# One-layer hybrid encoder block: the pages of the input stage in another order, its dependent steps further apart, a pool's tiles asked for in the old order

## The chip, the cores and the metric

One core of one Trainium2 chip runs the whole block. The metric is the device time of one execution in microseconds, the median of several runs. A core has a matrix engine (PE, whose weight loads are shown apart as PEld), a vector engine (DVE), a scalar engine (ACT), GpSimd (POOL) and a sync engine (SP). Here SP issues most of the loads, POOL issues the loads that add to what is in the tile, and PE, DVE and ACT do the arithmetic.

## The reference, cut to what matters

One layer on 512 tokens of width 2048. Only the first third bears on the change.

```python
h = rms_norm(x, norm_mix_w)
q_a, k_a, v_a, q_g, k_g, v_g, r_g, gate_lr = split_cols(h @ w_in, IN_SPLITS)
y_a = chunked_band_attention(q_a, k_a, v_a, att_rel_bias)        # 16 heads of 64
gate_logit = gate_lr @ w_gla_gate_up + b_gla_gate                # rank 16
log_a = log_sigmoid(gate_logit) / 16
o_g = gated_linear_attention(q_g, k_g, v_g, log_a)               # 4 heads, dv 256
y_g = rms_norm(o_g, gla_norm_w) * silu(r_g)
x = x + concat(y_a, y_g) @ w_out
# then a gated MLP with a causal convolution, and a gated embedding, unchanged here
```

The two values `v_a` and `v_g` are 512 x 1024 each. The per-token factor of `rms_norm` is not applied ahead of the products: they are made from `x * norm_mix_w`, and their results are scaled by the factor afterwards.

## The kernel before, in words

**Products.** Each large product is cut in quarters and made from seven products P1 to P7 instead of eight. Their left operands here are weights (L11, L12, L21, L22 from memory, and sums S1 to S4 of these), and their right operands are quarters of `x` and differences of them (R11, R21, R22, N1, N2, T3, T4). Float32 accuracy comes from splitting both factors into a high and a low float32r part and making three matmuls of them.

**The value stage** (lines 1004 to 1523) is the first of the kernel, and makes `v_g` and `v_a`. Its work is cut into 56 pages, `vpages` in line 1007: 14 steps, each one product of one value, with 4 pages. A page is 128 x 1024 weights, 512 KB. It takes an ACT copy that rounds it to the high part, a DVE subtraction that leaves the low part (`value_split`), and 12 matmuls of 128x512. Tiles named `wvg_..` and `wva_..` are raw pages, `w` is a split page, `in_R` and `in_N` are split operands of `x`, `h` holds split differences, and `vgA`, `vgB`, `vgC`, `vgD`, `vaA` and so on are the accumulators in PSUM (`VALUE_BANKS`, line 1006).

**Where a page comes from.** Pages of P1, P2 and P4 are plain loads by SP. The others hold sums of weights: SP loads L21 (`sum_load`; into the tiles e0 to e3 of the pool `gla` for `v_g`), and POOL issues a load of another block that is added to the tile on arrival (`sum_more`). One such tile is used three times, so the second sum can only be added after the split that read the first. In the trace these added loads are the queue q0, and those of SP are the queue q1.

**What sets the order.** `value_step(n)` (line 1049) issues the load of page n+4 where it is a plain one, splits page n+2, runs the functions that a table gives for step n (lines 1445 to 1501), and then issues the 12 matmuls of page n. The instructions stand on each engine in the order in which this code issues them. The table holds all that has to happen beside the products:

- `x_load` brings pieces of `x`; `left` and `right` split operands of it; `weigh_left`, `differences` and `spread_differences` make and split the others.
- `token_load` and `token_square` sum the squares of the tokens, and `token_norm` (step 26) makes of them the per-token factor: a root, its reciprocal and one Newton step on DVE (`rtok`), a diagonal of it (`dg`, four DVE operations in `rstd_bc`, line 136), a matmul that spreads it over the partitions (`pb`), and a copy to `rb`.
- `collect_first` and `collect_more` take accumulators out of PSUM, `value_done` scales a finished quarter by `rtok` on ACT and stores it to memory by POOL (`vgd`, `vad`).
- The gate of the linear attention: `gate_loads` (30) and `gate_weights` (34) load and split its weights (`g_S`, `gls`), `gate_rank` (35) multiplies them with `x` (64 matmuls, `plr`), `gate_low` (36) scales the result (`lf`, `lr`), `gate_up` (37, 39) makes the logits (`pz`), `gate_exp` and `gate_ln` (40, 41) the logarithm of their sigmoid, and sums, scans and decays follow (42 to 54).

**After the value stage** comes the front stage, with 16 units for the queries, keys and the output gate `r_g` (operand tiles `u`, accumulators `accA` to `accC`). The linear attention runs beside it, and its results are stored to memory as `ond` from the tiles `g_e` (line 1423). Then the pool `gla` is closed and the pool `att` of the softmax attention is opened on the same memory (`open_attention`, line 1533). A tile of the new pool waits for the last use of those tiles of the old one whose place it takes. `attend` (line 646) makes, for each pair of heads, the tiles Q, Kh and Kl (`high` on ACT, `low` on DVE), the scores (`psc` in PSUM), and the score tiles `sc` on DVE and ACT. Where a tile of the pool `gla` lies depends on the order in which its tags are first asked for: before, this was e0, e1, t9, e2, e3, t8, S.

**The output gate's units.** `after_gates` (line 758) multiplies a unit of `r_g` (128 x 1024) by the per-token factor on DVE, applies Silu on ACT and multiplies it by the linear attention's result.

Of the kernel before, what the change touches and what calls it, by code (L numbers as in the profile page):

```python
# [14 lines left out]
P = 128  # L15
# [27 lines left out]
def encoder_block(ctx: ExitStack, tc: tile.TileContext, A, out):  # L43
# [71 lines left out]
    def psum_aux(name):  # L115
        return aux_bank(name)
# [18 lines left out]

    def rstd_bc(rt):
        nt = rt.shape[1]
        dg = tp.tile([P, T], F32, tag="dg", name="dg")
        for t in range(nt):
            vec.tensor_scalar(dg[:, t * P:(t + 1) * P], ident, rt[:, t:t + 1], None, ALU.mult)  # L140
        pb = psum_aux("pb")[:, :nt * P]
        ten.matmul(pb, ones, dg[:, :nt * P], start=True, stop=True)
        return pb
# [739 lines left out]

    for i, f in enumerate(sum_chores(summed[:4])):
        agenda[11 + 5 * i].append((0, f))
# [121 lines left out]
    vpages = [(v, p, j) for v, p in VALUE_STEPS for j in range(4)]  # L1007
# [120 lines left out]

    def gate_loads():
# [32 lines left out]
    def x_load(kt, c):  # L1162
        syn.dma_start(xslot(kt, "")[:, c], A["x"][kt][:, c])
# [21 lines left out]
    mixed = {}  # L1185

    def differences(k, names):
# [3 lines left out]
        for name in names:  # L1191
# [4 lines left out]
            elif name == "N2":  # L1196
                place = ("sq", "dg", "acc", "sq", "dg", "sq", "acc", "dg")[k]
                mixed[k] = acc if place == "acc" else tp.tile([P, T], F32, tag=place, name="mixed")
# [26 lines left out]
    def token_norm():  # L1225
        token_roots(rtok)
        act.activation(rb, rstd_bc(rtok), AF.Copy)
# [216 lines left out]
    first_half, second_half = ("N1", "N2", "T4"), ("T4", "N2")  # L1444
    for n, *fs in (
            (0, (left, 2), (left, 3), *((x_load, k, hi_tokens) for k in (0, 1, 2))),
            (1, (left, 4), (left, 5), *((x_load, k, hi_tokens) for k in (3, 4, 5))),
            (2, (left, 6), (left, 7), *((x_load, k, hi_tokens) for k in (6, 7)), (x_load, 8, all_tokens)),
            (3, (x_load, 9, all_tokens), (x_load, 10, all_tokens), (weigh_left, 0), (weigh_left, 1)),
            (4, (x_load, 11, all_tokens), (x_load, 12, all_tokens), (differences, 0, first_half), (weigh_left, 2)),  # L1450
            (5, (x_load, 13, all_tokens), (x_load, 14, all_tokens), (right, 0, 0), (spread_differences, 0, *second_half), (right, 1, 0)),
            (6, (x_load, 15, all_tokens), (differences, 1, first_half), (weigh_left, 3)),
            (7, (right, 2, 0), (right, 3, 2), (spread_differences, 1, *second_half)),
            (8, (right, 4, 0), (right, 5, 0), (differences, 2, ("N1",)), (weigh_left, 4), (sum_load, "g", 0)),
            (9, (right, 6, 2), (right, 7, 2), (differences, 2, ("N2", "T4")), (weigh_left, 5)),
            (10, (spread_differences, 2, *second_half), (differences, 3, ("N1", "N2")), (weigh_left, 6), (sum_load, "g", 1)),
            (11, (differences, 3, ("T4",)), (spread_differences, 3, *second_half), (weigh_left, 7)),
            (12, (collect_first, "g", "C11", "A"), (collect_more, "g", "C11", "B"), (sum_load, "g", 2), (sum_more, "g", "P5", 0, "L22")),
            (13, (differences, 4, first_half), (sum_more, "g", "P5", 1, "L22")),
            (14, (spread_differences, 4, *second_half), (differences, 5, ("N1", "N2")), (sum_load, "g", 3)),  # L1460
            (15, (differences, 5, ("T4",)), (spread_differences, 5, *second_half), (sum_more, "g", "P5", 2, "L22")),
            (16, (differences, 6, first_half), (spread_differences, 6, "T4"), (sum_more, "g", "P5", 3, "L22"), (token_load, 0)),
            (17, (differences, 7, first_half), (spread_differences, 7, "T4"), (token_load, 1)),
            (18, (spread_differences, 0, "N1"), (spread_differences, 1, "N1"), (differences, 7, ("T3",)), (token_load, 2), (token_square, 0)),
            (19, (collect_first, "a", "C11", "A"), (collect_more, "a", "C11", "B"), (spread_differences, 2, "N1"),
             (differences, 3, ("T3",)), (spread_differences, 3, "N1", "T3"), (token_load, 3), (token_square, 1), (sum_more, "g", "P6", 0, "L11")),
            (20, (spread_differences, 4, "N1"), (spread_differences, 5, "N1"), (spread_differences, 7, "N1", "T3"), (differences, 6, ("T3",)), (token_load, 4), (token_square, 2),
             (sum_more, "g", "P6", 1, "L11")),
            (21, (collect_first, "g", "C21", "D", -1), (spread_differences, 6, "N1", "T3"),
             (token_load, 5), (token_square, 3), (sum_more, "g", "P6", 2, "L11")),  # L1470
            (22, *((differences, k, ("T3",)) for k in (0, 1, 2)), (token_load, 6), (token_square, 4), (sum_more, "g", "P6", 3, "L11")),
            (23, *((differences, k, ("T3",)) for k in (4, 5)), (token_load, 7), (token_square, 5), (sum_more, "g", "P3", 0, "L12")),
            (24, (collect_first, "g", "C22", "C", -1), (spread_differences, 6, "N2"), (spread_differences, 7, "N2"), (token_square, 6),
             (sum_more, "g", "P3", 1, "L12"), (value_load, "g", "P7", 0)),
            (25, (token_square, 7), (spread_differences, 0, "T3"), (spread_differences, 1, "T3"), (sum_more, "g", "P3", 2, "L12"),
             (value_load, "g", "P7", 1)),
            (26, (token_norm,), (right, 0, 1), (right, 1, 1), (sum_more, "g", "P3", 3, "L12"), (value_load, "g", "P7", 2),
             (sum_more, "g", "P7", 0, "L11")),
            (27, (right, 2, 1), (right, 4, 1), (value_done, "g", "C11"), (sum_more, "g", "P7", 1, "L11")),
            (28, (collect_first, "g", "C12", "A"), (right, 5, 1), (value_done, "a", "C11"), (use_rings, {"wr": ("r3", "r0", "r1", "r2")}),  # L1480
             (value_load, "g", "P7", 3), (sum_more, "g", "P7", 2, "L11")),
            (29, (spread_differences, 2, "T3"), (sum_load, "a", 0)),
            (30, (spread_differences, 4, "T3"), (spread_differences, 5, "T3"), (sum_more, "g", "P7", 3, "L11"), (gate_loads,)),
            (31, (sum_load, "a", 1)),
            (32, (collect_more, "g", "C12", "C"), (value_done, "g", "C12"), (sum_more, "a", "P5", 0, "L22")),
            (33, (sum_load, "a", 2)), (34, (gate_weights,), (sum_more, "a", "P5", 1, "L22")),
            (35, (gate_rank,), (sum_load, "a", 3)),
            (36, (collect_more, "g", "C21", "A"), (collect_more, "g", "C22", "A"), (value_done, "g", "C21"), (value_done, "g", "C22"),
             (gate_low,)),
            (37, (gate_up, (0, 1)), (gate_abs, (0, 1)), (gate_min, (0, 1))), (38, (sum_right, "a", 2)),  # L1490
            (39, (gate_up, (2, 3)), (gate_abs, (2, 3)), (gate_min, (2, 3)), (sum_right, "a", 3)),
            (40, (collect_first, "a", "C21", "D", -1), (gate_exp, (0, 1, 2, 3))), (41, (gate_ln, (0, 1, 2, 3))),
            (42, (gate_sum, (0, 1))), (43, (gate_scan, (0,)), (gate_sum, (2, 3))), (44, (collect_first, "a", "C22", "C", -1), (gate_scan, (1,))),
            (45, (gate_scan, (2,))), (46, (gate_scan, (3,))), (48, (collect_first, "a", "C12", "A")),
            (52, (collect_more, "a", "C12", "C"), (value_done, "a", "C12")),
# [4 lines left out]
            *((47 + i, (gate_decay, (i,))) for i in range(4)), *((51 + i, (gate_small, (i,))) for i in range(4)), (54, (linear_pages,)),  # L1500
# [6 lines left out]
    for k in (1, 2, 3):  # L1507
        x_load(k, lo_tokens)
    value_load("g", "P1", 1, 2)
    for k in (4, 5):  # L1510
        x_load(k, lo_tokens)
    value_load("g", "P1", 2)
    for k in (6, 7):
        x_load(k, lo_tokens)
# [3 lines left out]
    value_load("g", "P1", 3)  # L1518
# [284 lines left out]
```

## Time and profile before

| what | us |
|---|---|
| median of the runs (lowest and highest) | 2256.96 (2256.66 to 2257.14) |
| the profiled execution | 2257.45 |
| its span, first to last instruction | 2255.4 |
| PE busy in the span | 2188.2 (97%) |
| DVE, ACT, POOL busy | 1875.4, 1351.0, 227.1 |
| mean granted clock of PE | 0.986 |

The profiled execution is 0.5 us above the median, and 2.05 us of it lie outside the span. A row of a timeline gives the start, the time, the engine, the line, the operation, the result and operand tiles and the shape, with a count of equal instructions in a row; in brackets stands how long the engine sat idle ahead of it and what ended that. Nearly all rows name line 62, a helper that records every operation, so they are told apart by their tiles. A row of the windows gives the busy time of each engine in a stretch, the granted clock of PE as a share of full speed, and the busy share and rate of the DMA engines. The matrix engine is idle almost nowhere but in the value stage and at a few places of the front stage.

### The profile page before, as it was taken

What the parts mean: (1) busy time and instruction counts of PE and PEld (TensorE: products, weight loads), DVE (VectorE), ACT (ScalarE), POOL (GpSimd) and SP (SyncE); (2) the same over time, 40 slices, a digit from 0 to 9 for tenths busy, and PEclk for the clock granted to TensorE, in tenths of its full rate; (3) what the DMA queues carried; (4) which work ended last, traced back from release to release, by engine and by line L of the source; (5) the groups of instructions that cost most, each with busy time, mean ns of one, the idle gap of its engine ahead of it and who ended that gap; (6) DMA issues with size and microseconds to landing.
All of it is one profiled execution on the core that took longest, in us unless ns stands there. A gap on an engine that the chain in (4) does not pass through costs nothing.

```text
span 2255.4 us, 45743 instructions
## 1 busy us (share of the span) xinstructions
PE 2188.2 (97%) x18224; PEld 2134.9 (95%) x18224; DVE 1875.4 (83%) x2581; ACT 1351.0 (60%) x2018; POOL 227.1 (10%) x277
## 2 busy tenths in 40 slices
PE   8779998999999999999999999999999999999997
PEld 7568998899999999999999999999999999999997
DVE  6646787888778898999888888888888787898997
ACT  6647456777576575555555555555564464666765
POOL 0221101011010001111111110000000101000000
PEclk9889999999999999999999999999999999999998
DMA  9979787788998898999999997877876886979996
GB/s 301 254 200 219 212 228 213 213 230 242 263 350 255 272 320 235 293 300 296 291 285 289 271 253 222 212 226 212 233 292 164 257 240 171 337 239 338 292 295 200
DMA packets 205222, 576.08 MB, mean 255 GB/s; under 512 B 22384, under 2 KB 66672, under 8 KB 205008
## 3 DMA queue, kind: packets, MB, share of 16 engines
q1 hardware_dynamic: 166064, 437.70, 54.9%
q0 software_dynamic: 36960, 132.66, 31.1%
q8 instruction: 143, 2.34, 0.4%
q10 hardware_dynamic: 1984, 2.79, 0.3%
q14 instruction: 71, 0.58, 0.1%
HBM read 499.67 MB, written 119.54 MB: 275 GB/s over the span
## 4 chain that ended last, share of the span: by engine, by line
PE 74%; DVE 8%; DMA 8%; ACT 5%; issue 3%; SPq 0%; POOL 0%; DVEq 0%; ACTq 0%; POOLq 0%
PE accA L62 38%; PE accC L62 19%; PE accB L62 10%; DVE w L62 3%; ACT w L62 2%; PE vaA L62 1%; DVE u L62 1%; DMA wvg_P_r<-in_w_v_g 1%; DVE h L62 1%; DMA s<-in_w_up 1%; PE py L62 1%; PE vgA L62 1%; DMA ond<-g_e 1%; DVE s L62 1%; PE psc L62 1%
## 5 line engine op out<-in xcount | busy, mean ns | idle before, releaser
L62 PE MATMUL accA<-h,w 128*128 128x256 f32 x5088 | 615.9, 278 | 5.4 <-ACT u L62 4.5
L62 PEld LDWEIGHTS accA<-h,w 128*128 128x128 f32 x5088 | 596.8, 188 | 8.7 <-ACT u L62 5.4
L62 DVE TENSOR_TENSOR w<-s,w 128x1024 fp32r<-128x1024 f32 (+1 forms) x381 | 457.5, 1201 | 77.6 <-ACT w L62 76.8
L62 PE MATMUL accC<-h,w 128*128 128x256 f32 x4248 | 510.5, 277 | 0.0
L62 PEld LDWEIGHTS accC<-h,w 128*128 128x128 f32 x4248 | 495.6, 188 | 0.3
L62 DVE TENSOR_TENSOR w<-l,w 128x1024 fp32r<-128x1024 f32 (+1 forms) x320 | 382.9, 1196 | 64.2 <-ACT w L62 63.7
L62 ACT ACTIVATE w<-l 128x1024 fp32r<-128x1024 f32 (+1 forms) x320 | 332.1, 1039 | 172.0 <-PE accC L62 114.4
L62 ACT ACTIVATE w<-s 128x1024 fp32r<-128x1024 f32 (+1 forms) x381 | 394.8, 1037 | 22.2 <-PE accB L62 9.8
L62 ACT ACTIVATE u<-accA 128x256 f32<-128x256 f32 x302 | 114.1, 378 | 355.2 <-PE accA L62 355.1
L62 DVE TENSOR_TENSOR s<-s,l 128x1024 f32<-128x1024 f32 (+1 forms) x176 | 211.2, 1200 | 13.1 <-DMA s<-in_w_blk 8.6
L62 POOL DMA_DIRECT2D s<-in_w_up x84 | 73.0, 869 | 719.6 <-DMA s<-in_w_up 402.8
L62 DVE SCALAR_TENSOR_TENSOR cv<-u,cw,cv 128x511 f32<-128x511 f32 (+1 forms) x176 | 131.5, 747 | 3.1
L62 PE MATMUL accA<-up_R,w 128*128 128x256 f32 x1056 | 127.0, 276 | 0.0
L62 PE MATMUL accB<-up_R,w 128*128 128x256 f32 x1056 | 126.8, 276 | 0.0
L62 PE MATMUL accA<-up_N,w 128*128 128x256 f32 x1056 | 126.8, 276 | 0.1
L62 PEld LDWEIGHTS accA<-up_R,w 128*128 128x128 f32 x1056 | 123.0, 188 | 0.5 <-issue 0.5
L62 PEld LDWEIGHTS accA<-up_N,w 128*128 128x128 f32 x1056 | 122.9, 188 | 0.2 <-ACT u L62 0.2
L62 PEld LDWEIGHTS accB<-up_R,w 128*128 128x128 f32 x1056 | 123.1, 188 | 0.0
L62 DVE TENSOR_TENSOR u<-u,rb 128x1024 f32<-128x1024 f32 (+1 forms) x74 | 84.0, 1135 | 18.4 <-ACT u L62 18.2
L62 ACT ACTIVATE u<-accC 128x256 f32<-128x256 f32 x98 | 37.3, 380 | 95.9 <-PE accC L62 95.8
L62 ACT ACTIVATE cv<-u,cw 128x512 f32<-128x512 f32 x88 | 67.1, 810 | 29.7 <-DVE u L62 29.7
L62 DVE TENSOR_TENSOR u<-u,accC 128x256 f32<-128x256 f32 x102 | 42.6, 418 | 50.4 <-PE accC L62 50.0
(368 smaller groups left out, 2973.8 us busy)
## 6 DMA issues: line engine op xcount, KB each, us to landing
l<-in_w_up SPq DMA_DIRECT2D x132, 512.0 KB, 6.6
s<-in_w_up SPq DMA_DIRECT2D x84, 512.0 KB, 6.1
s<-in_w_up POOLq DMA_DIRECT2D x84, 512.0 KB, 7.8
l<-in_w_dn SPq DMA_DIRECT2D x56, 448.0 KB, 5.1
l<-in_w_blk SPq DMA_DIRECT2D x48, 512.0 KB, 5.5
s<-in_w_blk SPq DMA_DIRECT2D x32, 512.0 KB, 4.6
s<-in_w_blk POOLq DMA_DIRECT2D x32, 512.0 KB, 8.1
l<-in_w_out SPq DMA_DIRECT2D x28, 512.0 KB, 4.5
```

The source lines that it names most:

```text
L62: ins = f(*args, **kw)
```

## The change: what it does

**Pages of P1 in turn.** The first eight pages were four of `v_g` and then four of `v_a`; now they alternate. Since both values use the same two pieces of `x` for page j, the pieces are needed every second page. The first loads are reordered to match (x1, a page of `v_a`, x2, x3, a page of `v_g`), and the other pieces of `x` are spread over the steps 0 to 9.

**Dependent steps apart.** `token_norm` becomes four entries: the root and `rtok` at step 27, the diagonal at 28, the matmul `pb` at 30, the copy to `rb` at 32. The gate's weights go from step 34 to 36, its 64 matmuls from 35 to 39, `gate_low` from 36 to 41, `gate_up` from 37 and 39 to 43 and 45, exponential and logarithm from 40 and 41 to 48 and 49, the scans from 43 to 46 to 50 to 54. `value_done` of the first two quarters goes from 27 and 28 to 29 and 30, so on POOL the added loads of the P7 pages 0, 1 and 2 now stand ahead of their four stores, and that of page 3 stands behind them. Operands of later products are made later (`spread_differences` for N2, `right` for R22, and T3), and the tiles `mixed` lie elsewhere.

**Tiles in the old order.** All tags of the pool `gla` are asked for once at its start, in the order t9, t8, S, e0, e1, e2, e3.

**Output gate.** `scale_gate` multiplies three quarters of a unit of `r_g` by the per-token factor six steps into the unit, and `after_gates` is left with 128 x 256.

On PE, at the start of the value stage (`vgA` and `vaA` are the accumulators of P1 for `v_g` and `v_a`, `in_R` the two operand tiles for the pieces 0 to 3 and 4 to 7 of `x`):

```order
-L62 MATMUL vgA<-w,in_R_244 128x512 x24
-L62 MATMUL vgA<-w,in_R_284 128x512 x24
-L62 MATMUL vaA<-w,in_R_244 128x512 x24
-L62 MATMUL vaA<-w,in_R_284 128x512 x24
-L62 MATMUL vgB<-w,in_R_378 128x512 x12
+L62 MATMUL vgA<-w,in_R_246 128x512 x12
+L62 MATMUL vaA<-w,in_R_246 128x512 x12
+L62 MATMUL vgA<-w,in_R_246 128x512 x12
+L62 MATMUL vaA<-w,in_R_246 128x512 x12
+L62 MATMUL vgA<-w,in_R_305 128x512 x12
+L62 MATMUL vaA<-w,in_R_305 128x512 x12
```

The second operand tile was needed after 24 matmuls, and is now needed after 48.

On PE, further on, from the products P6 of `v_g` (`vgA<-w,h`) to the gate's matmuls (`plr`), before:

```order
L62 MATMUL vgA<-w,h_103 128x512 x24
L62 MATMUL pb<-dg,ones 128x512
L62 MATMUL vgA<-w,h_103 128x512 x24
L62 MATMUL vgC<-w,in_R_378 128x512 x12
L62 MATMUL vgC<-w,in_R_423 128x512 x12
L62 MATMUL vgC<-w,in_N_446 128x512 x12
L62 MATMUL vgC<-w,in_N_473 128x512 x12
L62 MATMUL vgA<-w,h_103 128x512 x36
L62 MATMUL plr<-in_R_244,g_S 128x256 x8
```

and now:

```order
L62 MATMUL vgA<-w,h_103 128x512 x48
L62 MATMUL vgC<-w,in_R_376 128x512 x12
L62 MATMUL vgC<-w,in_R_423 128x512 x12
L62 MATMUL pb<-dg,ones 128x512
L62 MATMUL vgC<-w,in_N_473 128x512 x12
L62 MATMUL vgC<-w,in_N_498 128x512 x12
L62 MATMUL vgA<-w,h_103 128x512 x48
L62 MATMUL vaD<-w,h_103 128x512 x36
L62 MATMUL plr<-in_R_246,g_S 128x256 x8
```

`pb` moved behind four more pages, and `plr` behind four more.

On DVE, in the softmax attention's first pair of heads, with what each row waits for (DMAHW is a load or store issued by SP or ACT), before:

```order
L62 SCALAR_TENSOR_TENSOR Q_3140<-u,Q_3140 64x512 [waits Activation_49]
L62 TENSOR_TENSOR Kl_3144<-u,Kh_3142 64x512 [waits DMAHW6_49,DMAHW5_49,Activation_49]
L62 SCALAR_TENSOR_TENSOR Q_3141<-u,Q_3141 64x512 [waits DMAHW0_49,Activation_49]
L62 TENSOR_TENSOR Kl_3145<-u,Kh_3143 64x512 [waits DMAHW4_49,Activation_49]
L62 TENSOR_TENSOR u<-u,accB 128x256 [waits PE_49]
L62 TENSOR_TENSOR s_3190<-s_3190,l_2972 128x1024 [waits DVE_49]
L62 ISA sc,mx<-psc,bias 128x512 [waits PE_49]
```

and now:

```order
L62 SCALAR_TENSOR_TENSOR Q_3165<-u,Q_3165 64x512 [waits Activation_49]
L62 TENSOR_TENSOR Kl_3169<-u,Kh_3167 64x512 [waits Activation_49]
L62 SCALAR_TENSOR_TENSOR Q_3166<-u,Q_3166 64x512 [waits DMAHW3_49,Activation_49]
L62 TENSOR_TENSOR Kl_3170<-u,Kh_3168 64x512 [waits DMAHW7_49,Activation_49]
L62 TENSOR_TENSOR u<-u,accB 128x256 [waits PE_49]
L62 TENSOR_TENSOR s_3215<-s_3215,l_2997 128x1024 [waits DVE_49]
L62 ISA sc,mx<-psc,bias 128x512 [waits DMAHW5_49,DMAHW4_49,PE_49]
```

The wait for two transfers (numbers 6 and 5 before, and 5 and 4 now, since the count is shifted by one) went from the first Kl to the first score tile, ten rows further on. On ACT the same two left the row of the second Kh. The rest of the instructions after the value stage, `scale_gate` aside, stand in the order in which they stood.

The diff, cut to its core:

```diff
-    vpages = [(v, p, j) for v, p in VALUE_STEPS for j in range(4)]
+    vpages = [(v, "P1", j) for j in range(4) for v in "ga"] + [(v, p, j) for v, p in VALUE_STEPS[2:] for j in range(4)]
...
+    for tag, cols_ in (("t9", 1024), ("t8", T), ("S", 768), *((f"e{i}", 1024) for i in range(4))):
+        gt(tag, cols_)
...
+    def scale_gate(unit):
+        vec.tensor_tensor(unit.o[:, 0], unit.o[:, 0], rb, ALU.mult)
+        vec.tensor_tensor(unit.o[:, 1, 256:T], unit.o[:, 1, 256:T], rb[:, 256:T], ALU.mult)
+
+    for u in front.units[12:]:
+        agenda[base[u] + 6].append((1, lambda u=u: scale_gate(u)))
...
-        return [(0, 0, load), (0, 1, lambda: vec.tensor_tensor(unit.o, unit.o, rb2, ALU.mult)),
+        r = rb[:, 0:256]
+        return [(0, 0, load), (0, 1, lambda: vec.tensor_tensor(unit.o[:, 1, 0:256], unit.o[:, 1, 0:256], r, ALU.mult)),
...
-    def token_norm():
-        token_roots(rtok)
-        act.activation(rb, rstd_bc(rtok), AF.Copy)
+    def token_spread():
+        G["dg"] = tp.tile([P, T], F32, tag="dg", name="dg")
+        for t in range(TT):
+            vec.tensor_scalar(G["dg"][:, t * P:(t + 1) * P], ident, rtok[:, t:t + 1], None, ALU.mult)
+
+    def token_bank():
+        G["pb"] = psum_aux("pb")
+        ten.matmul(G["pb"], ones, G["dg"], start=True, stop=True)
+
+    def token_out():
+        act.activation(rb, G["pb"], AF.Copy)
...
-            (26, (token_norm,), (right, 0, 1), (right, 1, 1), (sum_more, "g", "P3", 3, "L12"), (value_load, "g", "P7", 2),
...
+            (27, (token_roots, rtok), (differences, 3, ("T3",)), (differences, 0, ("T3",)), (sum_more, "g", "P7", 1, "L11")),
```

More of the change, by code (lines that the diff above doesn't have):

```diff
@@ L134, in token_roots @@
         vec.scalar_tensor_tensor(dst, t, 1.5, y, ALU.add, ALU.mult)
[L136 to L143, printed above, removed]
     w_all = hp.tile([P, 6 * 1024 + 136], F32R, name="w")
@@ L1443, in encoder_block, with x_rest @@
     lo_tokens, hi_tokens, all_tokens = slice(0, 256), slice(256, T), slice(0, T)
-    first_half, second_half = ("N1", "N2", "T4"), ("T4", "N2")
+    def x_rest(k):
+        x_load(k, hi_tokens)
+        x_load(k + 8, all_tokens)
     for n, *fs in (
[L1446 to L1464, printed above, removed]
@@ new lines, in encoder_block @@
+            (0, (left, 2), (left, 3), (x_load, 4, lo_tokens), (x_load, 5, lo_tokens)),
+            (1, (x_rest, 0)), (2, (left, 4), (left, 5), (x_load, 6, lo_tokens), (x_load, 7, lo_tokens)), (3, (x_rest, 1), (weigh_left, 0)),
+            (4, (x_rest, 2), (left, 6), (left, 7), (differences, 0, ("N1", "N2", "T4")), (weigh_left, 1)),
+            (5, (x_rest, 3), (right, 0, 0), (right, 1, 0), (spread_differences, 0, "T4", "N2")),
+            (6, (x_rest, 4), (differences, 1, ("N1", "N2", "T4")), (weigh_left, 2)),
@@ new lines, in encoder_block @@
+            (7, (x_rest, 5), (right, 2, 0), (right, 3, 0), (spread_differences, 1, "T4", "N2")),
+            (8, (x_rest, 6), (differences, 2, ("N1", "N2", "T4")), (weigh_left, 3)),
+            (9, (x_rest, 7), (right, 4, 0), (right, 5, 0), (spread_differences, 2, "T4"), (sum_load, "g", 0)),
+            (10, (right, 6, 0), (right, 7, 0), (differences, 3, ("N1", "N2")), (weigh_left, 4), (sum_load, "g", 1)),
+            (11, (differences, 3, ("T4",)), (differences, 4, ("N1", "N2")), (weigh_left, 5)),
@@ L1471, in encoder_block @@
[L1471 to L1476, printed above, removed]
@@ new lines, in encoder_block @@
+            (24, (spread_differences, 7, "N2"), (right, 1, 1), (differences, 7, ("T3",)), (token_square, 6), (sum_more, "g", "P3", 1, "L12"),
+             (value_load, "g", "P7", 0)),
+            (25, (collect_first, "g", "C22", "C", -1), (spread_differences, 7, "T3"), (right, 7, 1), (right, 2, 1), (token_square, 7),
+             (sum_more, "g", "P3", 2, "L12"), (value_load, "g", "P7", 1)),
+            (26, (right, 3, 1), (right, 4, 1), (right, 5, 1), (sum_more, "g", "P3", 3, "L12"), (value_load, "g", "P7", 2),
@@ L1487, in encoder_block @@
[L1487 to L1492, printed above, removed]
@@ new lines, in encoder_block @@
+            (38, (sum_right, "a", 2)), (39, (gate_rank,), (sum_right, "a", 3)),
+            (41, (collect_first, "a", "C21", "D", -1), (gate_low,)), (43, (gate_up, (0, 1))),
+            (45, (collect_first, "a", "C22", "C", -1), (gate_abs, (0, 1)), (gate_min, (0, 1)), (gate_up, (2, 3))),
+            (47, (gate_abs, (2, 3)), (gate_min, (2, 3))), (48, (gate_exp, (0, 1, 2, 3))),
+            (49, (collect_first, "a", "C12", "A"), (gate_ln, (0, 1, 2, 3)), (gate_sum, (0, 1))), (50, (gate_scan, (0,)), (gate_sum, (2, 3))),
@@ L1499, in encoder_block @@
             *((43 + j, (sum_more, "a", "P3", j, "L12")) for j in range(4)),
-            *((47 + i, (gate_decay, (i,))) for i in range(4)), *((51 + i, (gate_small, (i,))) for i in range(4)), (54, (linear_pages,)),
+            *((51 + i + (i > 1), (gate_decay, (i,))) for i in range(3)), (55, (gate_decay, (3,)), (gate_small, (0, 1, 2, 3))), (54, (linear_pages,)),
             *((n, (give, tag)) for n, tag in ((47, "r4"), (48, "r5"), (51, "r0"), (52, "r1"), (53, "r2"), (54, "r3")))):
@@ L1506, in encoder_block @@
     value_load("g", "P1", 0, 2)
[L1507 to L1514, printed above, removed]
+    x_load(1, lo_tokens)
+    value_load("a", "P1", 0)
+    x_load(2, lo_tokens)
+    x_load(3, lo_tokens)
+    value_load("g", "P1", 1)
     value_split(0, 2, lambda: left(0))
@@ L1517, in encoder_block @@
     value_split(1)
-    value_load("g", "P1", 3)
+    value_load("a", "P1", 1)
     for n in range(len(vpages)):
```

53 lines of the change are left out of this document (36 added, 17 removed).

## The prediction

> **What bounds the kernel now.** The page's first part gives PE 97% of the span, so time can only be won where PE stands still. The windows over the value stage come first (columns: stretch, length, busy time and count of PE, PEld, DVE, ACT, POOL, granted clock, DMA share, GB/s).
>
> ```profile
> 0.00:10.00 10.00, 7.43 (x34) 6.10 (x34) 2.61 (x6) 4.61 (x7) 1.44 (x11) 1.00 0.78 245
> 10.00:20.00 10.00, 6.77 (x20) 4.99 (x21) 5.16 (x8) 5.13 (x9) 0.00 (x0) 0.66 0.98 333
> 20.00:60.00 40.00, 40.00 (x178) 33.15 (x177) 33.60 (x50) 27.86 (x40) 3.58 (x4) 1.00 0.95 313
> 60.00:80.00 20.00, 15.18 (x59) 11.43 (x58) 15.05 (x26) 12.72 (x24) 2.55 (x3) 0.91 0.86 224
> 80.00:90.00 10.00, 10.00 (x46) 8.29 (x45) 8.24 (x12) 9.26 (x17) 3.10 (x4) 1.00 1.00 256
> 90.00:100.00 10.00, 0.98 (x5) 0.49 (x4) 4.99 (x14) 6.15 (x10) 2.01 (x3) 0.65 1.06 275
> 100.00:120.00 20.00, 20.00 (x80) 15.75 (x81) 9.30 (x13) 12.01 (x20) 6.32 (x8) 0.92 0.98 257
> 120.00:140.00 20.00, 11.51 (x52) 9.96 (x51) 7.70 (x10) 7.45 (x13) 3.34 (x4) 0.76 0.96 281
> 140.00:160.00 20.00, 15.31 (x80) 13.12 (x79) 7.44 (x10) 7.61 (x11) 5.35 (x8) 0.84 0.37 121
> 160.00:213.00 53.00, 51.97 (x224) 41.98 (x223) 33.87 (x44) 36.89 (x51) 12.40 (x15) 0.99 0.95 207
> ```
>
> Two things stand here at once. PE is idle and at a reduced clock in several stretches, and the DMA engines are nearly full in all but one (0.37 from 140 to 160). The timeline of PE names the stalls; the third row gives the full-speed price.
>
> ```profile
> 5.76 3.30 PE L62 MATMUL vgA<-w,in_R 128*128 128x512 f32 x12 [0.43 <-ACT in_R L62]
> 13.20 10.80 PE L62 MATMUL vgA<-w,in_R 128*128 128x512 f32 x36 [4.14 <-ACT in_R L62]
> 23.83 11.04 PE L62 MATMUL vaA<-w,in_R 128*128 128x512 f32 x48
> 34.71 5.60 PE L62 MATMUL vgB<-w,in_R 128*128 128x512 f32 x24
> ...
> 72.92 12.53 PE L62 MATMUL vgC<-w,h 128*128 128x512 f32 x48 [3.76 <-DVE g_t L62]
> ...
> 99.90 2.08 PE L62 MATMUL pb<-dg,ones 128*128 128x512 f32 x2 [9.02 <-DVE dg L62]
> ...
> 135.60 5.37 PE L62 MATMUL plr<-in_R,g_S 128*128 128x256 f32 x24 [8.49 <-DVE g_S L62]
> 140.81 1.12 PE L62 MATMUL plr<-in_N,g_S 128*128 128x256 f32 x8
> 141.77 1.10 PE L62 MATMUL plr<-in_R,gls 128*128 128x256 f32 x8
> ...
> 155.90 1.22 PE L62 MATMUL pz<-lr,g_t 128*128 128x512 f32 x2 [4.69 <-ACT lr L62]
> 156.92 7.66 PE L62 MATMUL vaD<-w,h 128*128 128x512 f32 x24
> 164.41 0.63 PE L62 MATMUL pz<-lr,g_t 128*128 128x512 f32 x2
> ...
> 213.12 2.90 PE L62 MATMUL accA<-in_R,w 128*128 128x256 f32 x24
> ```
>
> 48 matmuls take 34.71 - 23.83 = 10.88 us, so a page of 12 takes 2.72 and 56 pages 152.3. The gate's 64 `plr` matmuls cost about 7.7 (8 in 0.96), `pb` and `pz` about 1. That is 161 us of work between 5.76 and 213.12, which is 207.4: 46.4 us are lost. The five stalls above make 4.14 + 3.76 + 9.02 + 8.49 + 4.69 = 30.1 of it; the rest is mostly the clock after them (36 matmuls after the first took 10.63 us instead of 8.16).
>
> Three of the five are dependent steps set too close: `pb` waits for `dg`, made in the same step; `plr` for the gate's split weights; `pz` for `lr`, two steps after `plr`.
>
> The other large place is the first pair of heads of the softmax attention.
>
> ```profile
> 353.23 1.34 ACTq L1423 DMA_DIRECT2D ond<-g_e  x2
> ...
> 359.50 2.99 PE L62 MATMUL accA<-in_R,w 128*128 128x256 f32 x24
> 368.39 1.28 ACT L62 ACTIVATE Kh<-u 64x512 fp32r<-64x512 f32 x2 [10.38 <-DMA ond<-g_e]
> 368.43 0.68 DVE L62 TENSOR_TENSOR Kl<-u,Kh 64x512 fp32r<-64x512 f32 x1 [9.79 <-DMA ond<-g_e]
> ...
> 370.80 1.22 PE L62 MATMUL accB<-in_R,w 128*128 128x256 f32 x4 [8.31 <-ACT w L62]
> ...
> 376.09 0.46 PE L62 MATMUL psc<-Kh,Q 128*128 128x512 f32 x1
> ...
> 378.23 0.68 DVE L62 CUSTOM_DVE_ANT_0 sc<-psc,bias 128x512 f32<-128x512 f32 x1
> ```
>
> The new tiles Kh and Kl lie where `g_e` lay, whose store was issued at 353.23 and landed at 368.4. The page split for `accB` stands behind them on ACT, so PE waits 8.31 us, and the 24 matmuls of `accB` then take 5.29 us (370.80 to 376.09).
>
> **The change part by part.** *Pages in turn.* The second half of `in_R` is needed after four pages instead of two, 5.4 us later on PE. The 4.14 us stall and its clock go, and page 4 can start 5 us earlier (23.83 to about 18.5). But from 10 to 60 us the transfers run at 0.95 to 0.98, so PE then overtakes its pages and hands most of this back. I count none of it by itself.
>
> *Steps apart.* The diagonal itself is short:
>
> ```profile
> 98.97 0.88 DVE L62 TENSOR_SCALAR dg<-ident,rtok 128x128 f32<-128x128 f32 x4
> ```
>
> `pb` gets two steps between `dg` and itself (5.4 us; `dg` takes 0.88), `plr` three after the weights' split, `pz` two after `lr`. By PE alone 9.02, 8.49 and 4.69 go, and about 2 us of clock after each (24 matmuls after `pz` took 7.49 instead of 5.44). What each leaves behind: the same pages must have arrived earlier. So the stage's sum goes by the transfers.
>
> ```profile
> 0.00:213.00 213.00, 179.15 (x764) 145.25 (x765) 127.94 (x190) 129.68 (x197) 40.08 (x59) 0.91 0.89 245
> ```
>
> 0.89 of 213 is 189.6 us of DMA work, and the change removes no byte of it. In the long full stretches the share is 0.95 to 1.0. At 0.97 the work takes 195.5 us, so the stage ends 17.6 us earlier. Upper bound: no idle transfer at all, 23.4. Lower bound: only the stall whose stretch had free transfers, `pz`, goes: 4.69 and 2.05 of clock, 6.7. I take 17.6, since 0.95 is what the longest stretches without a large stall show (20 to 60, 160 to 213) and 0.98 to 1.06 those from 80 to 120. The free transfers that are left to fill lie almost all in the stretch at 0.37 (12.6 of the 23.4 us), which follows `plr` and holds `pz`.
>
> [...]
>
> *POOL's queue.* Before, the first stores of the values stood ahead of the added loads.
>
> ```profile
> 108.21 1.49 POOL L62 DMA_DIRECT2D vgd<-g_t  x2 [9.37 <-ACT g_t L62]
> 109.69 0.96 POOL L62 DMA_DIRECT2D wvg_P_r<-in_w_v_g  x1
> ```
>
> The load at 109.69 waited behind a store that waited 9.37 us for ACT. Now three of four go ahead, and only P7's page 3 stands behind four stores: it may come a few us late, once. Its cover is the two pages before it (5.4 us). It is inside the lower bound.
>
> *Added and moved work.* The gate's ACT and DVE operations come eight to nine steps later, between page splits, and number as many as before. `gate_exp` and `gate_ln` fall beside the collection of an accumulator at step 49; I take 0, bound 3 us, inside the 0.97. Its results are used after the stage.
>
> *Pool order.* Kh and Kl no longer wait. PE wins 8.31 and, at 2.72 for 24 matmuls, 2.57 of clock: 10.9. The same store is now waited for by `sc`. Without the stall `sc` would start at 378.23 - 10.9 = 367.3, and the store landed at 368.4. I subtract this 1.1 and another 0.8, since DVE's next page splits stand behind `sc`: 9. Bounds 6 (landing 4 us later) and 11.
>
> *Output gate.*
>
> ```profile
> 597.46 1.22 DVE L62 TENSOR_TENSOR u<-u,rb 128x1024 f32<-128x1024 f32 x1
> 598.71 1.06 ACT L62 ACTIVATE u<-u 128x1024 f32<-128x1024 f32 x1 [2.79 <-DVE u L62]
> 599.67 0.36 ACT L62 ACTIVATE u<-accA 128x256 f32<-128x256 f32 x1
> ...
> 600.09 4.27 PE L62 MATMUL accA<-h,w 128*128 128x256 f32 x24 [2.96 <-ACT u L62]
> ```
>
> Here PE waits 2.96 us for a chain that begins with 1.22 us on DVE; a quarter of that work remains, so 0.8 to 0.9 us go at this unit, little at the others. I take 1 (0 to 2: the clock after it may recover too). The three quarters done earlier fill DVE time beside PE.
>
> Sum: 17.6 + 9 + 1 = 27.6. From the profiled 2257.45 that is 2229.85, and as the median lies 0.5 below that execution, 2229.4.
>
> **The rivals.** *Transfers keep their time.* The first pages come sooner, but loads and added loads follow one another through few buffers, and the stage only wins the 6.7 us of `pz`. For it: shares of 0.95 to 1.06 beside the stalls of `pb` and `plr`. Against: PE's stall holds the buffers, so these transfers fetch ahead for later. 6.7 + 9 + 1 = 16.7: 2240.2. Chance 0.22.
>
> *Everything closes.* Transfers are never idle and the store has landed when `sc` comes: 23.4 + 11 + 2 = 36.4, 2220.5. Chance 0.12.
>
> *PE's own work binds.* If better order also made the transfers cheaper than 189.6, all 46.4 go: with 9 and 1, 2200.5. [...] Chance 0.02.
>
> *The store's wait moves.* The pages behind `sc` are fetched earlier, crowd the store of `ond`, and it lands 6 us later: the 9 become 3, 2235.4. Nothing of the landing on ACT's side is changed, which speaks against it. Chance 0.12.
>
> *No change.* `pb` and `plr` wait as long at the new places, since their inputs wait for the same late tokens and pages: within 4.5 us of before. Chance 0.03.
>
> *Slower: the clock.* PE, now ahead, waits for each page of steps 4 to 19, and stays at the low clock there. Price: 24 matmuls in 5.29 instead of 2.72, so 2.57 a page. It decides from (27.6 + 4.5) / 2.57 = 13 pages on; with all 16, 41 us are lost and the time is 2270. For it: after one 4.14 us gap the granted clock was 0.66 for a whole window. Against: PE was busy for 40.00 of 40 us from 20 to 60 at 0.95 of the transfers, so gaps there would be short. Chance 0.03.
>
> [...]
>
> **How the numbers follow.** The forecast has 0.46. The range runs from 2220.5 (upper bounds 23.4, 11 and 2) to 2244.3 (lower bounds 6.7, 6 and 0), rounded to 2220 and 2244.5; it holds the first, second and fourth case. 0.2%, about what a measurement of this kernel can tell, is 4.5 us. Faster by more: 0.46 + 0.22 + 0.12 + 0.02 + 0.12 = 0.94. Within: 0.03. Slower: 0.03.
>
> **What would show it.** Right: `accA` after the value stage starts near 195 instead of 213; `pb`, `plr` and `pz` wait under 1 us; the window that had 0.37 is at 0.9; Kh starts right after Q and `sc` waits for the store by 1 to 2 us. The first rival is right if the three waits are gone but PE waits as long for `w` (ACT, DVE, behind a load). Wrong altogether: `accA` starts after 207, or `accB` still waits over 5 us.

## The result, and the profile after

| | us |
|---|---|
| before, median of 4 (range) | 2257.05 (2256.66 to 2260.32) |
| changed, median of 4 (range) | 2232.44 (2231.36 to 2236.55) |
| ratio, 95% interval | 0.9891, 0.9874 to 0.9908 |
| the changed kernel's profiled execution, its span | 2236.55, 2234.8 |

The change saves 24.6 us (20.8 to 28.4 by the interval); 27.6 were forecast. Of the twelve runs of the pages in turn alone, below, three took 2430, 2443 and 12077 us, far longer than the other nine, and are left out of its median. The profiled execution is 4.1 us above the median of its runs, so its traces explain 20.6 us (span 2255.4 to 2234.8).

The windows of the changed kernel over the value stage, with the columns as before:

```profile
20.00:60.00 40.00, 39.79 (x176) 32.48 (x175) 34.05 (x56) 26.88 (x41) 3.59 (x4) 1.00 1.02 331
...
100.00:120.00 20.00, 15.55 (x60) 12.01 (x59) 8.89 (x14) 10.10 (x17) 6.29 (x9) 0.89 1.05 325
120.00:140.00 20.00, 20.00 (x115) 17.68 (x115) 13.37 (x16) 9.61 (x16) 8.49 (x12) 0.94 0.80 248
140.00:160.00 20.00, 14.83 (x66) 11.92 (x64) 8.62 (x8) 10.70 (x15) 4.20 (x5) 1.00 1.06 235
160.00:200.00 40.00, 37.03 (x157) 29.40 (x157) 23.19 (x25) 27.47 (x41) 6.49 (x8) 0.92 0.63 152
...
0.00:197.00 197.00, 176.96 (x764) 142.29 (x764) 125.20 (x186) 128.45 (x203) 39.42 (x59) 0.97 0.92 262
```

The transfers now run full from 20 to 120 us (1.05 and 1.06 from 60 to 100) and from 140 to 160 us; the share can read slightly above 1, so it is no exact measure. The stretch that had 0.37 is at 1.06, and the free time has moved to 120 to 140 us (0.80) and behind 160 us (0.63). The timeline of PE shows which waits went and which are new.

```profile
97.02 1.10 PE L62 MATMUL pb<-dg,ones 128*128 128x512 f32 x2 [1.70 <-DVE dg L62]
...
115.76 0.79 PE L62 MATMUL vgA<-w,h 128*128 128x512 f32 x1 [3.98 <-ACT w L62]
117.02 5.06 PE L62 MATMUL vgA<-w,h 128*128 128x512 f32 x11 [0.47 <-DVE w L62]
...
130.28 3.01 PE L62 MATMUL plr<-in_R,g_S 128*128 128x256 f32 x24
...
148.75 0.63 PE L62 MATMUL pz<-lr,g_t 128*128 128x512 f32 x2
...
160.92 1.45 PE L62 MATMUL pz<-lr,g_t 128*128 128x512 f32 x2 [6.09 <-DVE g_e L62]
...
197.39 3.00 PE L62 MATMUL accA<-in_R,w 128*128 128x256 f32 x24 [0.68 <-ACT w L62]
...
206.67 4.62 PE L62 MATMUL accA<-h,w 128*128 128x256 f32 x24 [3.56 <-ACT u L62]
211.13 2.89 PE L62 MATMUL accC<-h,w 128*128 128x256 f32 x24
```

`plr` and the first `pz` no longer wait, and `pb` waits 1.70 us instead of 9.02. Three waits are new: 3.98 us for P7's last page of `v_g`, 6.09 us at the second `pz`, and 3.56 us for `u` just after the stage, with a low clock behind it (24 matmuls in 4.46 us, to 211.13, at a granted clock of 0.62). `accA` starts 15.7 us earlier than before. Of this, 10.8 are left at `accC`, which before stood as in the first of these rows (timeline of PE, the kernel before; the second is a mark for the attention):

```profile
221.89 2.88 PE L62 MATMUL accC<-h,w 128*128 128x256 f32 x24
...
423.85 1.25 PE L62 MATMUL py<-PT,va 128*64 128x128 f32 x12 [0.80 <-ACT PT L62]
```

The softmax attention's beginning in the timeline of the changed kernel:

```profile
346.84 1.27 ACT L62 ACTIVATE Kh<-u 64x512 fp32r<-64x512 f32 x2
...
351.28 0.64 PE L62 MATMUL accB<-in_R,w 128*128 128x256 f32 x4
...
354.11 0.39 PE L62 MATMUL psc<-Kh,Q 128*128 128x512 f32 x1
...
357.53 0.69 DVE L62 CUSTOM_DVE_ANT_0 sc<-psc,bias 128x512 f32<-128x512 f32 x1 [0.23 <-DMA ond<-g_e]
...
376.96 1.25 PE L62 MATMUL py<-PT,va 128*64 128x128 f32 x12 [1.61 <-ACT PT L62]
...
404.77 1.25 PE L62 MATMUL py<-PT,va 128*64 128x128 f32 x12 [0.79 <-ACT PT L62]
```

Kh starts without a wait, `accB` follows at full speed (24 matmuls in 2.83 us, at a granted clock of 1.00), and `sc` waits 0.23 us for the store. At `psc` the kernel is 376.09 - 354.11 = 22.0 us ahead, at the `py` of 404.77 still 19.1: some 3 us come back in between, where PE waits for PT (1.61 instead of 0.76 us) and then runs 24 matmuls at a low clock (4.44 us instead of 2.86, at a granted clock of 0.62).

To compare kernels by their parts, three marks serve: the first `accA`, the first `accC`, and the `py` just shown, since whole times scatter. The kernel before ran from 2251.18 to 2264.32 us in the 17 runs beside the first experiments. The kernels of the table are explained in the experiments.

| profiled execution of | accA | accC | py |
|---|---|---|---|
| before | 213.12 | 221.89 | 423.85 |
| changed | 197.39 | 211.13 | 404.77 |
| changed, again | 197.23 | 210.97 | 404.19 |
| pool's order alone | 213.34 | 223.69 | 417.45 |
| pages in turn alone | 216.11 | 226.18 | 431.49 |
| steps apart alone | 200.25 | 213.99 | 416.12 |
| changed, output gate in one piece | 199.15 | 212.91 | 405.28 |
| changed, the gate's last steps later | 200.35 | 211.55 | 407.88 |

The last two run the changed kernel's code up to the last page of the value stage, so `accA` of one and the same stage wanders by 3 us, from 197.2 to 200.4. The products P6 of `v_g` already start at 76.6 to 80.5 us in the four profiles of this stage. From `accA` to `accC`, before and the pool's order alone have the same code too, and take 8.8 and 10.4 us. From `py` to the end of the span, where only the output gate differs, the eight take 1824.8 to 1832.4 us. The runs come from several chips; how much of this is the chip and how much chance stays open.

### The profile page after: what moved, and what is told of

It reads as the page before. It is cut to its first block, busy times and chain, and to the rows that moved or that the text cites. A ratio compares the mean times of both kernels' runs of the same rounds, so it can differ in the third digit from the quotient of the medians.

```text
span 2234.8 us, 45776 instructions
## 1 busy us (share of the span) xinstructions
PE 2186.1 (98%) x18224; PEld 2132.7 (95%) x18224; DVE 1876.8 (84%) x2599; ACT 1352.2 (61%) x2028; POOL 227.0 (10%) x277
## 4 chain that ended last, share of the span: by engine, by line
PE 78%; DVE 7%; DMA 7%; ACT 4%; issue 3%; POOL 0%; SPq 0%; DVEq 0%; ACTq 0%; POOLq 0%
PE accA L62 41%; PE accC L62 20%; PE accB L62 11%; DVE w L62 2%; ACT w L62 1%; DVE h L62 1%; DMA s<-in_w_blk 1%; DMA wvg_P_r<-in_w_v_g 1%; DVE u L62 1%; DMA g_e<-in_w_v_g 1%; PE psc L62 1%; PE py L62 1%; DMA ond<-g_e 1%; PE ptr L62 1%; PE po L62 1%
## 5 line engine op out<-in xcount | busy, mean ns | idle before, releaser
L62 DVE TENSOR_TENSOR u<-u,rb 128x1024 f32<-128x1024 f32 (+2 forms) x82 | 84.9, 1040 | 18.5 <-ACT u L62 18.3
```

The costliest lines, as they stand in the source:

```text
L62: ins = f(*args, **kw)
```

## The experiments

Theory: in the value stage the transfers set the pace, so a stall that goes is only worth the transfer time that was idle beside it. Rivals: the stalls simply add up; or one late transfer or one badly placed step is the bound.

**The changed kernel again.**

> The changed kernel once more, unaltered. Its profiled execution was 2236.55 us while the three others took 2231.4 to 2232.9. If the 4 us between them are a late page of the value stage, a second profile near 2232 us shows less waiting there (PE's waits at pz, 6.1 us, and at the last page of P7 of v_g, 4.0 us) and the same waits after the stage. If they are elsewhere, the waits of the value stage are the same within 1 us.

Measured: 2235.46 us, its profiled execution 2238.32. The waits of the stage are the same (6.39 at `pz`, 3.63 at P7's page, `accA` at 197.23). The marks repeat to 0.6 us here, though not in the other kernels with this stage. The second profile fell on the longest of its five executions again, so no profile shows one of the shorter ones, and where the 4 us between them lie stays open.

**Pool's order alone**, the only edit to the kernel before:

```diff
+    for tag, cols_ in (("t9", 1024), ("t8", T), ("S", 768), *((f"e{i}", 1024) for i in range(4))):
+        gt(tag, cols_)
```

> The kernel before with only the order in which the tiles of the pool gla are asked for. Theory (the store's wait goes from Kh and Kl to sc, where it is nearly over, but the pages behind the attention then come no earlier): PE's 8.3 us at accB go and about 3 us come back within the next 50 us, net 8 us, 2249 us. Rival 1 (all of it stays): 11 us, 2246 us. Rival 2 (the store's wait only moves, and what the changed kernel won there it won because the stage before it ended earlier): under 3 us, 2254 us or more.

Measured: 2245.39 us, ratio 0.9949 (0.9934 to 0.9965). The timeline of PE:

```profile
362.96 2.88 PE L62 MATMUL accA<-in_R,w 128*128 128x256 f32 x24
365.69 0.62 PE L62 MATMUL accB<-in_R,w 128*128 128x256 f32 x4
...
417.45 1.25 PE L62 MATMUL py<-PT,va 128*64 128x128 f32 x12 [0.71 <-ACT PT L62]
```

`accB` follows `accA` at once. From `accC` to `py` it wins (423.85 - 221.89) - (417.45 - 223.69) = 8.2 us; the changed kernel wins 8.3 there. So the wait did not just move, and the part is independent of the stage. All the kernels bear it out: with the order of before, the profiles take 202.0 to 205.3 us from `accC` to `py`, and with the new one 191.1 to 193.8, where the gate's last steps don't fall between. The theory's 8 holds; the 11.5 us of the whole time fit the first rival, but by the marks 3 of them are from elsewhere.

**Pages in turn alone** (the edit is the line of `vpages`, the first loads and the steps 0 to 9 for pieces of `x`):

> The kernel before with only the pages of P1 in turn and the first loads to match; the dependent steps stay close. Theory (transfers set the pace from 10 to 130 us, so PE overtakes its pages and waits later instead): the first stall of 4.1 us goes, the stall at pb grows by about as much, and under 2 us are left, 2255 to 2257 us. Rival (stalls simply add): 6 us, 2251 us.

Measured: 2259.35 us (nine runs), ratio 1.0009 (0.9996 to 1.0022).

```profile
18.18 2.88 PE L62 MATMUL vgA<-w,in_R 128*128 128x512 f32 x12
...
41.42 2.89 PE L62 MATMUL vgB<-w,in_N 128*128 128x512 f32 x6 [2.58 <-ACT in_N L62]
...
73.25 7.07 PE L62 MATMUL vgC<-w,h 128*128 128x512 f32 x18 [3.75 <-DVE g_t L62]
...
100.23 2.08 PE L62 MATMUL pb<-dg,ones 128*128 128x512 f32 x2 [7.67 <-DVE dg L62]
```

The fifth page starts at 18.18 instead of 23.83, yet `vgC` starts at 73.25 (before 72.92): all of it is given back within 55 us, first at a wait for a late piece of `x`. `accA` is 3 us later than before, as much as it wanders in the changed stage. Nothing is gained alone, as the theory says, though the stall at `pb` shrank rather than grew.

**Steps apart alone** (the changed kernel with the old order of P1, of the pool's tiles and of the output gate):

> The changed kernel with P1 in the old order and the old first loads, the pool's tiles in the order of before, and the output gate as before: only the dependent steps are apart. Theory (transfers bind, and the steps apart let them run through): most of the stage's gain is here, accA after the stage starts 10 to 14 us earlier than before, and 4 to 5 us come back at once at the gate's late operations, net 7 to 10 us, 2247 to 2250 us. Rival 1 (stalls add): 20 us or more, 2237 us. Rival 2 (steps apart only pay together with the pages in turn): under 4 us, 2253 us or more.

Measured: 2246.38 us, ratio 0.9945 (0.9931 to 0.9959).

```profile
200.25 3.02 PE L62 MATMUL accA<-in_R,w 128*128 128x256 f32 x24 [0.68 <-ACT w L62]
209.54 4.62 PE L62 MATMUL accA<-h,w 128*128 128x256 f32 x24 [3.55 <-ACT u L62]
```

12.9 us at `accA`, 7.9 left at `accC`: the theory's figures (the whole time is 0.6 us under its range). The pages in turn beside it would be worth 200.25 - 197.39 = 2.9 us, but `accA` of the changed stage alone wanders by as much, so no worth of theirs is shown.

**Half of the added bytes**, in the changed kernel and in the one before; the right halves of these sums lack their second block, so neither kernel computes the layer:

```diff
-        pool.dma_start(raw, value_page(v, name, j), accum_op=ALU.add)
+        pool.dma_start(raw[:, 0:512], value_page(v, name, j)[:, 0:512], accum_op=ALU.add)
```

> The changed kernel, where every load of the value stage that adds to a tile (30 pages) adds only the left half of its columns; the right half of those sums lacks its second block. That takes 30 x 0.25 MB = 7.9 MB or about 38 us out of the 189.6 us of transfers (4.9 us a MB on POOL's queue). Theory (the transfers set the stage's pace until about 160 us): the waits for late pages go (P7's last page 3.6 to 4.0, pz 6.1 to 6.4, most of the small ones), and accA after the stage starts at 180 to 185 instead of 197; about 10 to 15 us less in all. Rival (the waits left are dependent steps too close, whatever arrives): accA still starts after 193.

> The kernel before with the same half sums. Theory (before, the dependent steps pb, plr and pz stop PE whatever arrives): the three waits of 9.0, 8.5 and 4.7 us stay to more than half, and accA starts at 200 or later instead of 213, so the same bytes are worth no more here than in the changed kernel. Rival (before, too, everything waits for transfers): the waits shrink under 3 us each and accA starts below 190.

Measured: 2220.88 us (ratio to before 0.9835, 0.9817 to 0.9854) and 2253.14 us (0.9981, 0.9968 to 0.9993). First the changed kernel with half sums:

```profile
149.91 0.49 PE L62 MATMUL pz<-lr,g_t 128*128 128x512 f32 x1 [3.48 <-DVE g_e L62]
...
185.63 3.09 PE L62 MATMUL accA<-in_R,w 128*128 128x256 f32 x24 [0.68 <-ACT w L62]
```

and the kernel before with half sums:

```profile
95.82 2.08 PE L62 MATMUL pb<-dg,ones 128*128 128x512 f32 x2 [6.87 <-DVE dg L62]
...
132.07 5.49 PE L62 MATMUL plr<-in_R,g_S 128*128 128x256 f32 x24 [8.37 <-DVE g_S L62]
...
152.75 1.22 PE L62 MATMUL pz<-lr,g_t 128*128 128x512 f32 x2 [4.69 <-ACT lr L62]
...
210.18 2.90 PE L62 MATMUL accA<-in_R,w 128*128 128x256 f32 x24
```

The same bytes are worth 11.6 us at `accA` in the changed kernel, and 2.9 before, no more than `accA` of the changed stage wanders. Before, `pb`, `plr` and `pz` keep nearly their whole waits: steps too close were the bound there. After the change the transfers bind, though not alone, since 27 us of transfers fewer (0.83 of 186 us against 0.92 of 197; 38 were expected) gave 11.6. The second `pz` still waits 3.48 us.

**The second `pz` two steps later**:

```diff
-(gate_abs, (0, 1)), (gate_min, (0, 1)), (gate_up, (2, 3))),
+(gate_abs, (0, 1)), (gate_min, (0, 1))),
-(47, (gate_abs, (2, 3)), (gate_min, (2, 3))),
+(47, (gate_up, (2, 3)), (gate_abs, (2, 3)), (gate_min, (2, 3))),
```

> The changed kernel with the second pair of the gate's logits two steps later (gate_up of heads 2 and 3 from step 45 to 47). In the changed kernel PE waits 6.1 to 6.4 us there, since the two banks are freed on ACT and DVE behind the split of page 47, which arrives late, while pages 45 and 46 are ready. Theory (this wait is the step's place, and the transfers have free time behind it, share 0.63): the wait falls under 2 us, accA starts 4 to 5 us earlier, at 192 to 193. Rival (transfers bind here too): PE waits as long for the pages 47 and 48, accA within 1.5 us of 197.

Measured: 2230.57 us (0.9879, 0.9864 to 0.9895), against 2235.46 for the changed kernel in its five runs.

```profile
162.97 0.51 PE L62 MATMUL pz<-lr,g_t 128*128 128x512 f32 x1 [0.82 <-DVE g_e L62]
...
191.63 3.10 PE L62 MATMUL accA<-in_R,w 128*128 128x256 f32 x24 [0.67 <-ACT w L62]
```

The wait is 0.82 us, and `accA` is 5.6 to 5.8 us earlier than in the changed kernel. From the first `pz` (here at 150.44) to `accA` it takes 41.2 us, and 48.6 to 49.4 in four profiles that have this stretch unaltered, so some 7 us are won there with no byte less: the step's place. The whole times alone would not tell, since the intervals of the two ratios overlap. The trace of the changed kernel shows the coupling on ACT and DVE:

```profile
157.47 1.06 ACT L62 ACTIVATE w<-wva_s 128x1024 fp32r<-128x1024 f32 x1 [1.49 <-DMA wva_s<-in_w_v_a]
158.44 1.06 ACT L62 ACTIVATE vaC<-vaC 128x512 f32<-128x512 f32 x2
159.39 1.27 ACT L62 ACTIVATE g_e<-pz,cols 128x512 f32<-128x512 f32 x2
160.11 1.41 DVE L62 TENSOR_SCALAR g_e<-pz,cols 128x512 f32<-128x512 f32 x2 [0.33 <-ACT g_e L62]
```

The operations that free the banks stand behind the split of the page two ahead, so PE's page 45 waited for page 47 to arrive, and then 160.92 - 157.47 = 3.5 us for the split and the operations behind it. This agrees with the 3.48 us that remained with half of the added bytes.

**P7's last page sooner**: its buffer freed and its load issued at step 27 instead of 28, its added load ahead of the stores.

> The changed kernel with page 3 of the product P7 of v_g loaded one step earlier (its buffer is freed one step earlier by making T3 of piece 0 first) and its added load ahead of the four stores on POOL. Theory (the transfers are full there, share 1.05, so what comes first only makes something else late): the wait of 3.6 to 4.0 us for this page shrinks, but accA starts at most 2 us earlier. Rival (the load behind the stores costs all of the wait and the slow clock after it): accA starts 6 to 7 us earlier, at 190 to 191.

Measured: 2238.58 us (0.9917, 0.9904 to 0.9931), `accA` at 201.98, 4.6 us later than in the changed kernel.

```profile
115.03 2.83 PE L62 MATMUL vgA<-w,h 128*128 128x512 f32 x11 [0.76 <-DVE w L62]
...
124.54 0.49 PE L62 MATMUL vaD<-w,h 128*128 128x512 f32 x1 [1.69 <-ACT w L62]
```

The wait for this page is gone, and the pages behind it are late instead. The rival (6 to 7 us won) falls, and the theory (a win of 2 us at most) holds. A loss is not shown: P6's first page, two steps ahead of the edit, already starts at 80.48 us instead of 76.94, so only 1 to 2 us of the 4.6 arise behind it, and the interval of the whole time overlaps that of the changed kernel (0.9883 to 0.9914).

**The gate's last steps in the front stage**, alone and with the second `pz` later:

```diff
-(55, (gate_decay, (3,)), (gate_small, (0, 1, 2, 3))),
+(55, (gate_small, (0,))),
+    agenda[6].append((1, lambda: gate_decay((3,))))
+    agenda[7].append((1, lambda: gate_small((1, 2, 3))))
```

> The changed kernel with the gate's last steps (decay of head 3, the small decays of heads 1 to 3) six and seven steps into the front stage instead of at the value stage's last page. In the changed kernel accA waits there for ACT's u by 3.4 to 3.6 us, and the 24 matmuls after it run at a low clock (4.62 us). Theory (these gate operations stand on DVE and ACT ahead of the last collection and of u): the wait falls under 1.5 us, and accC<-h after it starts 3 to 5 us earlier, near 207, with accA still at 197. Rival (the collection of the last accumulators itself is late, since the stage's end is now closer to it): the wait stays over 2.5 us.

> The changed kernel with both edits: the second pair of logits at step 47 and the gate's last steps in the front stage. Theory (two separate waits): accA at 191 to 192 and accC<-h 3 to 5 us closer behind it, in all 8 to 10 us less than the changed kernel, 2225 to 2227 us. Rival (the second only hides the first): no more than the 5 us of the first, 2230 us.

Measured: 2236.40 us (0.9902, 0.9879 to 0.9925) and 2226.54 us (0.9862, 0.9842 to 0.9882). With both edits:

```profile
191.05 3.01 PE L62 MATMUL accA<-in_R,w 128*128 128x256 f32 x24 [0.68 <-ACT w L62]
199.32 4.62 PE L62 MATMUL accA<-h,w 128*128 128x256 f32 x24 [2.54 <-ACT u L62]
203.78 2.88 PE L62 MATMUL accC<-h,w 128*128 128x256 f32 x24
```

Alone, `accA` to `accC` takes 211.55 - 200.35 = 11.2 us instead of 13.7; with both it takes 12.7. The wait for `u` only falls from 3.56 to 2.56 us alone and 2.54 with both, so these gate operations are less than a third of it. The rival (over 2.5 us) holds, barely, and the theory (under 1.5) falls; what makes the rest of the wait is not shown. The difference of 1.5 us between the two is the clock behind nearly the same wait: 24 matmuls took 2.93 us alone and 4.46 with both, as long as in the changed kernel at a granted clock of 0.62. Alone, `accA` was 3 us late, at 200.35; P6 of `v_g` started 2.6 us late already (79.52 us), long before the edit, so this is how far the stage wanders. With both, 2226.54 us is what the theory gave (2225 to 2227), and the lowest time of a kernel that computes the whole, 30 us below before.

**The output gate in one piece.**

> The changed kernel with the output gate's scaling in one piece, as before. Theory (a shorter chain ahead of Silu): PE's wait for u at the last unit of the gate, 2.1 to 2.3 us, becomes 2.9 to 3.2, so 0.8 us. Rival (the pieces made no difference): within 0.3 us. The whole time cannot tell, only the trace.

Measured: 2234.21 us (0.9895, 0.9865 to 0.9925).

```profile
572.38 1.23 DVE L62 TENSOR_TENSOR s<-s,l 128x1024 f32<-128x1024 f32 x1 [0.59 <-DMA s<-in_w_blk]
...
578.61 1.22 DVE L62 TENSOR_TENSOR u<-u,rb 128x1024 f32<-128x1024 f32 x1
...
581.24 3.00 PE L62 MATMUL accA<-h,w 128*128 128x256 f32 x24 [1.88 <-ACT u L62]
```

and the changed kernel at the same place:

```profile
571.66 1.23 DVE L62 TENSOR_TENSOR s<-s,l 128x1024 f32<-128x1024 f32 x1 [1.51 <-DMA s<-in_w_blk]
...
578.02 0.42 DVE L62 TENSOR_TENSOR u<-u,rb 128x256 f32<-128x256 f32 x1
...
579.85 4.56 PE L62 MATMUL accA<-h,w 128*128 128x256 f32 x24 [2.13 <-ACT u L62]
```

From the last scaling to PE the chain is 0.8 us shorter in pieces (1.83 instead of 2.63 us), as costed, but PE waits 2.13 us, not less than the 1.88 in one piece. By PE's wait the rival holds. But the wait also depends on when the page for `s` lands, at which DVE's chain begins. From that row to PE it takes 8.86 us in one piece (581.24 - 572.38) and 8.19 in pieces (579.85 - 571.66), and the other profiles agree: 8.85 to 8.87 in the six kernels with one piece, 8.19 to 8.20 in the seven profiles with pieces. So the pieces are worth 0.67 us, and here a page that landed later against PE's work hid it.

## Why the prediction was right, and where it was off

- **The stage goes by the transfers: right in part, and the number in part by luck.** Forecast were 17.6 us and `accA` near 195; it starts at 197.39, 15.7 us earlier. The half sums show that bytes bind in the changed kernel and hardly did before, but the second `pz`, set later, shows that a step's place bound as well. The sum was 189.6 us of transfers at a share of 0.97. The trace has a share of 0.92 over 197 us, so 181 us of transfers: the share was taken too high and the transfer time too, and the two errors nearly cancel. At 0.92 the 189.6 us would have ended at 206. Of the 8 us, about 2.4 are bytes that move behind `accA` (an estimate: 0.49 MB less by then on POOL's queue, which before took 45.2% of 213 us for 19.54 MB); the rest stays open. With the second `pz` later, the share is 0.95 up to `accA`, close to the 0.97.
- **A reading of the windows was wrong.** The 12.6 us at the share of 0.37 are little more than half of the 23.4 that were free, not almost all of them; the rest lay in the first 10 us, from 20 to 80 and behind 160 us. It does not enter the sum.
- **Pages in turn count for nothing by themselves: right.** Alone they win nothing, and beside the steps apart no more than the stage wanders.
- **`pb`, `plr` and `pz` stop waiting: right for `plr` and the first `pz`.** `pb` still waits 1.70 us, more than the 1 us named, and the second `pz` 6.09 us, which were not foreseen. The step taken was to count the distance from `lr` to `pz` and not from the second `pz` to what frees its banks.
- **P7's page 3 a few us late, once: right in kind**, 3.98 us of waiting and about 2.6 of clock (11 matmuls from 117.02 to 121.88 at a granted clock of 0.50, 4.9 us instead of 2.5, and 0.2 behind). The cover named, two pages, was gone. Bringing it forward did not help.
- **The gate's late operations at 0, bound 3: the mis-sized term.** Behind `accA` 15.7 - 10.8 = 5.0 us are given back, at the wait for `u` and its clock (3.4 against the kernel with the pool's order alone, whose code is that of before up to there). So the stage is worth 10.8 us, not 17.6; that lies above the lower bound of 6.7. The experiment moves 1 to 2.5 us of it away.
- **Pool's order, 9 (6 to 11): right.** 8.3 us, with 11.2 at first (up to `psc`) and 3 given back at PT, which was not named. `sc` waits 0.23 us where 1.1 were reckoned.
- **Output gate, 1 (0 to 2): right.** The chain is 0.67 us shorter; in this profile a later page hides it from PE.

By the marks that is 10.8 + 8.3 = 19.1 at `py`, and 20.6 at the end. The medians say 24.6 in the first runs and 21.5 (2256.91 to 2235.46) in the later ones; executions scatter by as much, part of it in code that is the same. So the 24.6 come nearer to the forecast's 27.6 than what the traces show of its parts. Of the rivals, the one that the transfers keep their time came closest: the stage's net gain lies between its 6.7 and the forecast's 17.6. The slower clock in the first pages did not occur (1.00 from 20 to 60 us).

## What to carry to other kernels

Add up what the transfers need in a stage before adding up its stalls: in this stage PE came out 15.7 us earlier, within the 23.4 us in which the transfers lay idle and far from the 46.4 of stalls and clock. Where a step frees a bank for PE, look at what stands ahead of it on its engine: here it was the split of a page that PE needs two pages later, and PE waited 6.09 us. The order in which a pool's tiles were asked for decided here whose store the later pool's tiles waited for (8.2 us from `accC` to `py`, by that edit alone), and the wait put further down the chain cost next to nothing (0.23 us). Before a few microseconds are put down to an edit, see whether they stand in the trace ahead of the place where the edit acts.

## What the runs showed of the hardware

A low clock came after gaps of 1.61 and 2.20 to 2.22 us, and not each time. In the changed kernel the 1.61 us wait for PT was followed by 24 matmuls in 382.58 - 378.14 = 4.44 us, at a granted clock of 0.62:

```profile
378.14 4.60 PE L62 MATMUL accA<-in_R,w 128*128 128x256 f32 x24
```

The same wait in the kernel with the gate's last steps later was followed by 24 matmuls in 384.62 - 381.77 = 2.85 us, at a clock of 1.00:

```profile
380.60 1.25 PE L62 MATMUL py<-PT,va 128*64 128x128 f32 x12 [1.60 <-ACT PT L62]
381.77 3.01 PE L62 MATMUL accA<-in_R,w 128*128 128x256 f32 x24
```

In the value stage, six profiles of kernels with the same code up to there wait 2.20 to 2.22 us ahead of the products P5 of `v_g`. The 48 matmuls after it took 11.0 us at a clock of 1.00 in three of them (the changed kernel twice, the gate's last steps later), and 12.6 to 13.8 us at 0.78 to 0.86 in the other three (the output gate in one piece, P7's page sooner, the second `pz` later). This is part of what `accA` wanders. So in these rows the length of the gap alone did not decide.
